# Two mixers of a float32 transformer: the input's projections as plain float32 matmuls instead of split ones

## The chip, the cores and the metric

The kernel runs on one core of one Trainium2 chip. The metric is the device time of one execution in microseconds (us). A core has five engines with a queue each: TensorE (PE in the rows; PEld is its weight load), VectorE (DVE), ScalarE (ACT), GpSimd (POOL) and SyncE (SP), whose queue issues nearly all DMAs here. Matmul results land in PSUM, in eight banks of 128x512 float32; everything else lies in SBUF.

## The reference, cut to what matters

A batch of one, 256 tokens of width 1024, float32 throughout. Two layers of a first block are followed by a second block that the change does not touch. Each layer of the first block is

```
mix = hybrid_mixer(x, w_in[l], ...)
x = layer_norm(ALPHA * x + mix)
ff = swiglu(x) if l == 0 else moe_swiglu(x)
x = layer_norm(ALPHA * x + ff)
```

and the mixer begins with one projection of its input, `proj = einsum('btd,de->bte', x, w_in)`, whose 3218 columns are cut into the queries, keys, values, decay, beta and gate of a gated delta rule (chunks of 64 tokens, 6 heads of 64), the two halves of a gated linear unit before a depthwise convolution over 31 tokens, and the queries, keys, values and forget gates of a causal attention. The three results are joined and multiplied by an output matrix.

## The kernel before

**Stages.** `build` runs mixer 0, a dense feed-forward, mixer 1 (both by `mixer1`), a mixture of experts, and the second block. Weights are packed on the host so that 1 MB (128 partitions x 2048 floats) is one DMA. `load` (L162) takes one of four `raw` slots in turn and issues that DMA on SP's queue, for all stages.

**The split.** TensorE has a one-pass form for operands rounded to float32r. To keep float32 accuracy, every operand is written as high + low part. `part` (L169) makes, from one half of a raw block, `wh` on ScalarE (L172, a copy that rounds) and `wl` on VectorE (L174, raw minus `wh`); three buffers of each. `mm3` (L181) then multiplies by three matmuls, high x high (L183), high x low (L184) and low x high (L185). The input is transposed by TensorE in `split_t` (L255) and split in the same way: `xTh` by ScalarE (L271), `xTl` by VectorE (L272).

**The projections in a mixer.** `proj_a` (L212) gives channels on partitions: per block two tiles of 128 channels, each eight groups of `mm3` over the 1024 inputs, with the weights stationary and 256 tokens moving. `proj_b` (L224) gives tokens on partitions: the input stationary, 256 weight columns moving. `proj_s` (L241) does as `proj_a` for the 18 small columns. A mixer has 19 channel tiles (`TILES_A`: k, q, v, the attention's f and g, and b and a of the gated linear unit), three blocks by `proj_b` (attention values, gates) and one by `proj_s`. All results go through two PSUM banks with the tag "a".

**Order of the work.** The source traces `proj_s`, three `pair_in` (k and q), `decays`, `pair_front`, `spare(3)` and `spare(4)` (values and one attention tile), then `inverse`, `scan`, `fox`, `conv` and `gates`. The framework's scheduler turns the trace into one order per engine: an instruction that is ready goes, and among ready ones the earlier in the source. So the projections in `fox`, `conv` and `gates` fill TensorE while the inverse waits for VectorE (`invert16`, L509 and L510: 15 dependent steps). Each engine then runs its list strictly in order.

**Near the change.** `conv` already multiplies plain float32 on TensorE: some of its 31 taps are diagonal 128x128 matrices against 256 tokens (`mm` at L362, tile `a_conv`); the other taps are VectorE's (L764). At the end of a mixer `split_t` makes the two parts `mT` of the joined result, which take the same buffers as `xTh` and `xTl`, and `proj_b` multiplies them by the output matrix, as before the change and after it.

Of the kernel before, what the change touches and what calls it, by code (L numbers as in the profile page):

```python
# [9 lines left out]
F32 = mybir.dt.float32  # L10
# [10 lines left out]
P = 128  # L21
D = 1024
KC = D // P
T = 256
# [79 lines left out]
class Net:  # L104
# [107 lines left out]
    def proj_a(self, src, xT, tiles=2, parts=None):  # L212
# [8 lines left out]
                self.mm3(ps[:, t, :], wh[:, k, :], wl[:, k, :], xh[:, k, :], xl[:, k, :], k == 0, k == 7)  # L221
        return ps

    def proj_b(self, src, xT, cols=256, nk=8, parts=None):  # L224

        xh, xl = xT
        ps = self.ps("a", "pB").rearrange("p (t n) -> p t n", t=2)
        k0 = 0
        for wh, wl in parts or self.weights(src, nk * cols):
            wh = wh.rearrange("p (k c) -> p k c", c=cols)  # L230
            wl = wl.rearrange("p (k c) -> p k c", c=cols)
            n = wh.shape[1]
            for t in range(2):
                for k in range(n):
                    s = slice(t * P, t * P + P)
                    self.mm3(ps[:, t, :cols], xh[:, k0 + k, s], xl[:, k0 + k, s], wh[:, k, :], wl[:, k, :],
                             k0 + k == 0 and t == 0, k0 + k == nk - 1)
            k0 += n
        return ps

    def proj_s(self, tag, src, xT, cols, sb):  # L241

        xh, xl = xT
        (wh, wl), = self.weights(src, 8 * cols)
        wh, wl = (w.rearrange("p (k c) -> p k c", c=cols) for w in (wh, wl))
        ps = self.ps("a", "pS")
        for k in range(8):
            self.mm3(ps[:cols, :T], wh[:, k, :], wl[:, k, :], xh[:, k, :], xl[:, k, :], k == 0, k == 7)
        self.nc.scalar.activation(sb, ps[:cols, :T], AF.Copy)
        ps = self.ps(tag, "pSt").rearrange("p (t n) -> p t n", t=2)  # L250
        for t in range(2):
            self.nc.tensor.transpose(ps[:, t, :cols], sb[:, t * P:t * P + P], self.ident[:cols, :cols])
        return ps[:, :, :cols]

    def split_t(self, tag, x, hl, kcs, gains=None, src0=0):  # L255

        nc = self.nc
        hi, lo = hl
        kcs = list(kcs)
        step = 2  # L260
        for b in range(0, len(kcs), step):
            sub = kcs[b:b + step]
            ps = self.ps(tag, "tr").rearrange("p (k t n) -> p k t n", k=2, t=2)
            for i, kc in enumerate(sub):
                for t in range(2):
                    o = (src0 + kc - kcs[0]) * P
                    nc.tensor.transpose(ps[:, i, t, :], x[:, t, o:o + P], self.ident)
            if gains is None:
# [85 lines left out]
    def mixer1(self, l, x, xT):  # L354
        nc, A, ident = self.nc, self.A, self.ident
        V, S, PE = nc.vector, nc.scalar, nc.tensor
        wA, wB, wS = A["w_in_a"], A["w_in_b"], A["w_in_s"]
# [12 lines left out]
        ps = self.proj_s("g", wS[l], xT, 18, mp.tile([18, T], F32, name="projs", tag="rowf"))  # L370
# [20 lines left out]
        ps = self.ps("g", "cum").rearrange("p (t n) -> p t n", t=2)  # L391
# [11 lines left out]
        rows = mp.tile([18, 2, T], F32R, name="rowsT")  # L403
        ps = self.ps("g", "rows")
# [24 lines left out]

        def pair_in(p):  # L430

            psj = self.proj_a(wA[l, p], xT)
            kq = kqs[p] = mp.tile([P, 2, T], F32, name=f"kq{p}")
            for i in range(2):
                conv4(kq[:, i, :], psj[:, i, :], 3 * i + p)
            sg = mp.tile([P, 2, T], F32, name="sg", bufs=3)
            self.sigmoid(sg, kq)
            V.tensor_tensor(kq, kq, sg, op=ALU.mult)
# [173 lines left out]
        def spare(c):  # L612

            names = TILES_A[2 * c:2 * c + 2]
            ps = self.proj_a(wA[l, c][:, :1024 * len(names)], xT, tiles=len(names))
            for i, n in enumerate(names):
                if n[0] == "v":
                    value(ps[:, i, :], int(n[1]))
                else:
                    S.activation({"b": glu[:, 0:2], "a": glu[:, 2:4], "f": foxqk[:, 0:3], "g": foxqk[:, 3:6]}[n[0]][:, int(n[1]), :],  # L620
                                 ps[:, i, :], AF.Copy)
# [12 lines left out]
        def fox():  # L634

            for c in FOXC:
                spare(c)
                yield
            ps = self.proj_b(wB[l, 0], xT)
            S.activation(fv[:, :, 0:256], ps, AF.Copy)  # L640
            yield
            ps = self.proj_b(wB[l, 1], xT)
            S.activation(fv[:, :, 256:384], ps[:, :, 0:128], AF.Copy)
            S.activation(gate[:, :, 0:128], ps[:, :, 128:256], AF.Copy)
            yield
            for t in range(2):
                n = P * (t + 1)
# [138 lines left out]

        def gates():
            gsg = late[3]
            ps = self.proj_b(wB[l, 2], xT)
            S.activation(gate[:, :, 128:384], ps, AF.Copy)  # L790
            self.sigmoid(gsg, gate)
            V.tensor_tensor(gate, gate, gsg, op=ALU.mult)
            yield
# [6 lines left out]
        for c in range(2):  # L800
            g = msc[:, 3 + c:4 + c]
# [37 lines left out]
        self.normed = self.rsqrt(rs, mv[:, :, 1], 1.0, 1e-5)  # L839
        return mv, rs  # L840

    def layer_norm_T(self, tag, r, st, rows, n=4):

        V = self.nc.vector
        mv, rs = self.moments(r, st, n)
        xT = self.new_xT()
        for h in range(2):
            s = slice(h * 512, h * 512 + 512)
            for t in range(2):
                V.scalar_tensor_tensor(r[:, t, s], r[:, t, s], mv[:, t, 0:1], rows[:, 0, s], op0=ALU.subtract, op1=ALU.mult)  # L850
                V.scalar_tensor_tensor(r[:, t, s], r[:, t, s], rs[:, t:t + 1], rows[:, 1, s], op0=ALU.mult, op1=ALU.add)
            self.split_t(tag, r, xT, range(4 * h, 4 * h + 4), src0=4 * h)
        return xT

    def layer_norm_T_first(self, tp, tag, r, st, rows, name, n=4):

# [35 lines left out]
        return r  # L892

    def to_T(self, tag, x):
        xT = self.new_xT()
        self.split_t(tag, x, xT, range(8))
        return xT

    def residual_ffn1(self, fp, l, x, xT, spare):
        A, nc = self.A, self.nc  # L900
# [951 lines left out]
def build(tc, A, out):  # L1852
    with ExitStack() as ctx:
# [13 lines left out]
            r, st = net.residual_ffn1(fp, 0, r, xT, net.prepare2(fp))  # L1867
        with net.banks(a=2, g=4, f=2), pool("mix1") as net.mp:
            rows = net.load_rows(net.mp.tile([P, 2, D], F32, name="rows", tag="lb"), "ln_ffn", 0, 2)
            xT = net.layer_norm_T("g", r, st, rows, 2)  # L1870
            r, st = net.mixer1(1, r, xT)
        with net.banks(a=4, y=2, t=2), pool("moe") as fp:
            rows = net.load_rows(fp.tile([P, 2, D], F32, name="rows"), "ln_mix", 2, 2)
# [34 lines left out]
```

## Time and profile before

| | us |
|---|---|
| median of 3 runs (2184.49 to 2192.83) | 2185.77 |
| the profiled execution, its own time | 2192.82 |
| its span, first to last instruction | 2191.0 |
| TensorE matmul busy in the span | 2060.1 |
| VectorE busy | 1294.7 |
| ScalarE busy | 1024.0 |
| mean granted TensorE clock, share of full | 0.968 |

The profile is one execution, recorded by the hardware. A row of a window gives, for each engine, the busy time and the count of its instructions; PEclk is the granted clock of TensorE as a share of 2.4 GHz. Matmuls overlap, so their durations add up to more than the time that they take; the distance between two starts tells what one costs. A row of the waits names the engine, line and tile that waited, and what released it.

### The profile page before, as it was taken

The numbers are of one execution on the slowest core, as the hardware profiler recorded it, in microseconds if no ns is written. First come the engines' busy times: TensorE is split into PE (matmuls) and PEld (weight loads), VectorE is DVE, ScalarE is ACT, GpSimd is POOL, SyncE is SP. The second block draws the span as 40 slices with busy tenths as digits, with TensorE's granted clock in tenths as the row PEclk, the third lists the DMA queues.
The fourth block names the chain that finished last, engine by engine and source line by source line (L and its number), as shares of the span: only waits on it lengthen the run. The fifth ranks groups of instructions, "written<-read, shape, count | busy, mean of one in ns | idle before, by whom it ended". The sixth has DMA issues, their size and how long they took to land. (4 is left out here: it accounts for less than half of the span.)

```text
span 2191.0 us, 31905 instructions
## 1 busy us (share of the span) xinstructions
PE 2060.1 (94%) x12770; PEld 1610.7 (74%) x12770; DVE 1294.7 (59%) x1903; ACT 1024.0 (47%) x1448; POOL 13.0 (1%) x27
## 2 busy tenths in 40 slices
PE   8998999899979999998899999987799999999998
PEld 7877999788768888432377785322699988878997
DVE  6768954666668998300288985000555568665554
ACT  6445444464547777200177774000544444554443
POOL 0000000000000000000000000000000000000000
PEclk9979999998989999999999999999899999999999
DMA  6313675322459999899999999999455553444552
GB/s 234 106 40 117 216 259 175 135 87 98 167 188 338 359 340 352 321 425 425 426 426 417 348 347 364 425 426 424 182 183 191 180 196 126 135 163 154 179 187 97
DMA packets 78988, 545.36 MB, mean 249 GB/s; under 512 B 8961, under 2 KB 11273, under 8 KB 13937
## 3 DMA queue, kind: packets, MB, share of 16 engines
q1 hardware_dynamic: 76112, 527.40, 64.2%
q0 software_dynamic: 2720, 15.84, 1.9%
q8 instruction: 103, 1.69, 0.3%
q14 instruction: 53, 0.43, 0.1%
HBM read 536.72 MB, written 6.49 MB: 248 GB/s over the span
## 5 line engine op out<-in xcount | busy, mean ns | idle before, releaser
L174 DVE TENSOR_TENSOR wl<-raw,wh 128x1024 fp32r<-128x1024 f32 (+1 forms) x662 | 799.2, 1218 | 378.5 <-ACT wh L172 375.0
L172 ACT ACTIVATE wh<-raw 128x1024 fp32r<-128x1024 f32 (+1 forms) x662 | 694.2, 1055 | 602.8 <-PE a_pA L184 272.8
L183 PE MATMUL a_pA<-xTh,wh 128*128 128x256 f32 x1456 | 420.7, 290 | 6.2 <-ACT foxqk L620 3.5
L185 PE MATMUL a_pA<-xTh,wl 128*128 128x256 f32 x1456 | 416.7, 287 | 0.7 <-DVE wl L174 0.7
L184 PE MATMUL a_pA<-xTl,wh 128*128 128x256 f32 x1456 | 417.1, 287 | 0.2 <-DVE xTl L875 0.2
L183 PEld LDWEIGHTS a_pA<-xTh,wh 128*128 128x128 f32 x1456 | 282.4, 194 | 14.8 <-ACT foxqk L620 5.6
L184 PEld LDWEIGHTS a_pA<-xTl,wh 128*128 128x128 f32 x1456 | 282.6, 194 | 4.9 <-issue 3.2
L185 PEld LDWEIGHTS a_pA<-xTh,wl 128*128 128x128 f32 x1456 | 282.4, 194 | 3.6 <-issue 2.4
L1032 PE MATMUL a_up<-raw,xef 128*64 128x512 f32 x896 | 218.8, 597 | 26.3 <-DMA raw<-in_moe_w_dram 26.2
L1037 DVE TENSOR_TENSOR mos<-mos,a_up 128x512 f32<-128x512 f32 x42 | 28.7, 683 | 267.6 <-PE a_up L1032 258.7
L1032 PEld LDWEIGHTS a_up<-raw,xef 128*64 128x64 f32 x896 | 68.5, 136 | 154.9 <-issue 105.4
L184 PE MATMUL a_up<-wl,xeh 128*128 128x512 f32 x448 | 180.3, 403 | 1.9 <-DVE wl L174 1.8
L185 PE MATMUL a_up<-wh,xel 128*128 128x512 f32 x448 | 178.0, 397 | 0.0
L183 PE MATMUL a_up<-wh,xeh 128*128 128x512 f32 x448 | 175.8, 399 | 0.0
L183 PE MATMUL a_pB<-wh,xTh 128*128 128x256 f32 x480 | 140.9, 295 | 5.6 <-ACT glu L620 3.2
L184 PE MATMUL a_pB<-wl,xTh 128*128 128x256 f32 x480 | 139.0, 290 | 0.0
L1065 PE MATMUL y_y<-raw,mof 128*64 128x512 f32 x448 | 131.8, 600 | 7.5 <-DMA raw<-in_moe_w_dram 7.4
L185 PE MATMUL a_pB<-wh,xTl 128*128 128x256 f32 x480 | 137.7, 289 | 1.1 <-DVE xTl L278 0.9
L184 PEld LDWEIGHTS a_up<-wl,xeh 128*128 128x128 f32 x448 | 84.7, 189 | 28.3 <-DVE wl L174 6.8
L1036 ACT ACTIVATE mos<-a_up 128x512 f32<-128x512 f32 x42 | 24.7, 587 | 171.0 <-PE a_up L1032 168.7
L185 PE MATMUL acc_acc<-wh,ffl 128*128 128x512 f32 x264 | 102.0, 392 | 0.0
L184 PE MATMUL acc_acc<-wl,ffh 128*128 128x512 f32 x264 | 102.0, 392 | 0.0
(559 smaller groups left out, 2774.0 us busy)
## 6 DMA issues: line engine op xcount, KB each, us to landing
raw<-in_moe_w_dram SPq DMA_DIRECT2D x336, 1024.0 KB, 10.8
raw<-in_ffn_in_dram SPq DMA_DIRECT2D x44, 1024.0 KB, 4.9
raw<-in_ffn_w_dram SPq DMA_DIRECT2D x33, 1024.0 KB, 4.9
raw<-in_w_in_a_dram SPq DMA_DIRECT2D x24, 1024.0 KB, 4.9
raw<-in_ffn_out_dram SPq DMA_DIRECT2D x22, 1024.0 KB, 4.9
raw<-in_w_out_dram SPq DMA_DIRECT2D x12, 1024.0 KB, 4.9
raw<-in_w_in_g_dram SPq DMA_DIRECT2D x12, 1024.0 KB, 5.0
raw<-in_w_in_b_dram SPq DMA_DIRECT2D x6, 1024.0 KB, 4.9
```

Of the source, the lines that this page charges most:

```text
L172: nc.scalar.activation(wh[:, :m], raw[:, o:o + m], AF.Copy)
L174: nc.vector.tensor_tensor(wl[:, :m], raw[:, o:o + m], wh[:, :m].bitcast(F32), op=ALU.subtract)
L183: mm(out, lh, rh, start=start, stop=False, skip_group_check=True)
L184: mm(out, lh, rl, start=False, stop=False, skip_group_check=True)
L185: mm(out, ll, rh, start=False, stop=stop, skip_group_check=True)
L1032: PE.matmul(ps[r], xe[0][:, k0, r], w[:, k * 512:k * 512 + 512], start=k0 == 0, stop=k0 == 7, skip_group_check=True)
L1036: self.last = S.activation(s, pp[0], AF.Silu)
L1037: V.tensor_tensor(s, s, pp[1], op=ALU.mult)
L1065: PE.matmul(py[h][r], hf[:, k, r], w[:, j * 1024 + h * 512:j * 1024 + h * 512 + 512], start=b == 0 and k == 0, stop=b == 6 and k == 3, ski ...
```

## The change

In both mixers every projection of the input takes the raw weight block and an unsplit transposed input, as plain float32 operands: one matmul in place of three, and no `part`. `plain_a`, `plain_b` and a second branch in `proj_s` do this; `to_T` and `layer_norm_T(..., flat=True)` make the one transposed input `xTf`, in the buffer of `xTl`, with its copies alternately on VectorE and ScalarE. The output projection of the mixers, the feed-forward, the experts and the second block keep the split form.

```diff
+    def plain_a(self, src, xf, tiles=2):
+
+        raw = self.load(src, 1024 * tiles).rearrange("p (t k c) -> p t k c", t=2, k=8)
+        ps = self.ps("a", "pA").rearrange("p (t n) -> p t n", t=2)
+        for t in range(tiles):
+            for k in range(8):
+                self.nc.tensor.matmul(ps[:, t, :], raw[:, t, k, :], xf[:, k, :], start=k == 0, stop=k == 7, skip_group_check=True)
+        return ps
+
+    def plain_b(self, src, xf):
+
+        raw = self.load(src).rearrange("p (k c) -> p k c", k=8)
+        ps = self.ps("a", "pB").rearrange("p (t n) -> p t n", t=2)
+        for t in range(2):
+            for k in range(8):
+                self.nc.tensor.matmul(ps[:, t, :], xf[:, k, t * P:t * P + P], raw[:, k, :], start=k + t == 0, stop=k == 7, skip_group_check=True)
+        return ps
...
+            w = self.load(src, 8 * cols)[:, :8 * cols].rearrange("p (k c) -> p k c", c=cols)
+            for k in range(8):
+                self.nc.tensor.matmul(ps[:cols, :T], w[:, k, :], xT[:, k, :], start=k == 0, stop=k == 7, skip_group_check=True)
...
+            if lo is None:
+                (nc.scalar.copy if b % 4 else nc.vector.tensor_copy)(hi[:, sub[0]:sub[0] + len(sub), :], ps[:, :len(sub)].rearrange("p k t n -> p k (t n)"))
...
-            psj = self.proj_a(wA[l, p], xT)
+            psj = self.plain_a(wA[l, p], xT)
...
-            ps = self.proj_a(wA[l, c][:, :1024 * len(names)], xT, tiles=len(names))
+            ps = self.plain_a(wA[l, c][:, :1024 * len(names)], xT, len(names))
...
-            ps = self.proj_b(wB[l, 0], xT)
+            ps = self.plain_b(wB[l, 0], xT)
...
-            ps = self.proj_b(wB[l, 1], xT)
+            ps = self.plain_b(wB[l, 1], xT)
...
-            ps = self.proj_b(wB[l, 2], xT)
+            ps = self.plain_b(wB[l, 2], xT)
...
-        xT = self.new_xT()
-        self.split_t(tag, x, xT, range(8))
+        xT = self.flat_xT()
+        self.split_t(tag, x, (xT, None), range(8))
         return xT
+
+    def flat_xT(self):
+        return self.ap.tile([P, 8, T], F32, name="xTf", tag="xTl")
...
-            xT = net.layer_norm_T("g", r, st, rows, 2)
+            xT = net.layer_norm_T("g", r, st, rows, 2, flat=True)
```

## Rows read from the trace of the kernel before

**Rows 1.** Windows of both mixers: length; busy PE, PEld, DVE, ACT, POOL; clock, DMA, GB/s.

```profile
9.80:176.50 166.70, 157.70 (x1445) 133.13 (x1443) 118.76 (x286) 89.71 (x197) 0.86 (x2) 0.91 0.30 107
415.70:584.10 168.40, 161.30 (x1453) 136.31 (x1451) 113.61 (x268) 88.88 (x195) 0.53 (x1) 0.89 0.26 89
```

**Rows 2.** Windows of 10 us, columns as above.

```profile
60.00:70.00 10.00, 8.42 (x67) 7.44 (x60) 9.97 (x28) 1.60 (x3) 0.00 (x0) 0.83 0.31 107
80.00:90.00 10.00, 8.42 (x70) 8.22 (x70) 8.73 (x28) 6.29 (x14) 0.00 (x0) 1.00 0.31 107
120.00:130.00 10.00, 10.00 (x71) 6.44 (x71) 4.88 (x14) 2.78 (x10) 0.00 (x0) 0.55 0.01 2
130.00:140.00 10.00, 10.00 (x86) 7.07 (x82) 5.23 (x17) 3.94 (x15) 0.00 (x0) 0.50 0.00 1
140.00:150.00 10.00, 10.00 (x87) 7.78 (x88) 5.07 (x16) 3.96 (x13) 0.00 (x0) 0.59 0.01 2
...
540.00:550.00 10.00, 10.00 (x70) 6.77 (x64) 4.03 (x12) 4.21 (x15) 0.00 (x0) 0.50 0.01 2
```

**Rows 3.** Waits of TensorE in mixer 1: total us, times, longest.

```profile
PE a_pA L183 <- ACT foxqk L620: 1.8, 2, 1.6
PE a_pB L183 <- ACT glu L620: 1.6, 1, 1.6
PE f_cvar L362 <- ACT glu L772: 1.2, 1, 1.2
PE a_pA L183 <- ACT wh L172: 1.2, 1, 1.2
PE g_tr L267 <- DVE mixed L816: 0.9, 2, 0.6
```

**Rows 4.** Line 183 in mixer 1: ns min/median/max, first and last start.

```profile
L183 PE MATMUL a_pA<-xTh,wh x152: 275/283/682, 416.1 to 524.8; 128*128 128x256 f32 x152
...
L183 PE MATMUL a_pB<-wh,xTh x49: 278/283/563, 495.8 to 584.1; 128*128 128x256 f32 x49
...
L183 PE MATMUL a_pS<-xTh,wh x8: 276/282/562, 415.7 to 420.4; 128*18 128x256 f32 x8
```

**Rows 5.** Timeline of TensorE in mixer 0, ends of a run: start, us.

```profile
21.18 0.28 PE L183 MATMUL a_pA<-xTh,wh 128*128 128x256 f32 x1
...
25.38 0.28 PE L185 MATMUL a_pA<-xTh,wl 128*128 128x256 f32 x1
```

**Rows 6.** The same timeline around one tap of the convolution.

```profile
160.37 0.28 PE L185 MATMUL a_pB<-wh,xTl 128*128 128x256 f32 x1
160.49 0.59 PE L362 MATMUL a_conv<-cup,dgt 128*128 128x256 f32 x2
160.74 0.47 PE L183 MATMUL a_pB<-wh,xTh 128*128 128x256 f32 x1
161.04 0.28 PE L184 MATMUL a_pB<-wl,xTh 128*128 128x256 f32 x1
```

**Rows 7.** Windows of lines 174 (VectorE), 172 (ScalarE) alone, mixer 1.

```profile
415.70:584.10 168.40, 31.77 (x26) 0.89 0.26 89
...
415.70:584.10 168.40, 27.49 (x26) 0.89 0.26 89
```

**Rows 8.** VectorE's groups in mixer 0: count, busy us, mean ns.

```profile
L272 DVE TENSOR_TENSOR xTl<-g_tr,xTh 128x512 fp32r<-128x512 f32 x4 | 2.8, 690 | 1.3 <-ACT xTh L271 1.3
```

**Rows 9.** DMA issues: count, size, median us from issue to landing.

```profile
raw<-in_w_in_a_dram SPq DMA_DIRECT2D x24, 1024.0 KB, 4.9
```

**Rows 10.** Windows of the inverse's steps: line 174 alone, then all engines.

```profile
80.50:105.90 25.40, 7.33 (x6) 1.00 0.42 131
...
80.50:105.90 25.40, 23.82 (x189) 22.54 (x189) 21.60 (x61) 12.17 (x25) 0.00 (x0) 1.00 0.42 131
```

**Rows 11.** Weight loads: line 183 in mixer 1, line 362 in both.

```profile
L183 PEld LDWEIGHTS a_pA<-xTh,wh x152: 186/192/338, 415.9 to 524.7; 128*128 128x128 f32 x152
...
L362 PEld LDWEIGHTS a_conv<-cup,dgt x56: 186/192/337, 122.4 to 574.7; 128*128 128x128 f32 x56
```

More of the change, by code (lines that the diff above doesn't have):

```diff
@@ L241, in proj_s @@
     def proj_s(self, tag, src, xT, cols, sb):
-        xh, xl = xT
-        (wh, wl), = self.weights(src, 8 * cols)
-        wh, wl = (w.rearrange("p (k c) -> p k c", c=cols) for w in (wh, wl))
         ps = self.ps("a", "pS")
-        for k in range(8):
-            self.mm3(ps[:cols, :T], wh[:, k, :], wl[:, k, :], xh[:, k, :], xl[:, k, :], k == 0, k == 7)
+        if isinstance(xT, tuple):
+            xh, xl = xT
+            (wh, wl), = self.weights(src, 8 * cols)
+            wh, wl = (w.rearrange("p (k c) -> p k c", c=cols) for w in (wh, wl))
+            for k in range(8):
+                self.mm3(ps[:cols, :T], wh[:, k, :], wl[:, k, :], xh[:, k, :], xl[:, k, :], k == 0, k == 7)
+        else:
+            w = self.load(src, 8 * cols)[:, :8 * cols].rearrange("p (k c) -> p k c", c=cols)
+            for k in range(8):
+                self.nc.tensor.matmul(ps[:cols, :T], w[:, k, :], xT[:, k, :], start=k == 0, stop=k == 7, skip_group_check=True)
         self.nc.scalar.activation(sb, ps[:cols, :T], AF.Copy)
@@ L267, in split_t @@
                     nc.tensor.transpose(ps[:, i, t, :], x[:, t, o:o + P], self.ident)
-            if gains is None:
+            if lo is None:
+                (nc.scalar.copy if b % 4 else nc.vector.tensor_copy)(hi[:, sub[0]:sub[0] + len(sub), :], ps[:, :len(sub)].rearrange("p k t n -> p k (t n)"))
+            elif gains is None:
                 k0, n = sub[0], len(sub)
@@ L840, in moments, with layer_norm_T @@
         return mv, rs
-    def layer_norm_T(self, tag, r, st, rows, n=4):
+    def layer_norm_T(self, tag, r, st, rows, n=4, flat=False):
         V = self.nc.vector
         mv, rs = self.moments(r, st, n)
-        xT = self.new_xT()
+        xT = (self.flat_xT(), None) if flat else self.new_xT()
         for h in range(2):
@@ L852, in layer_norm_T @@
             self.split_t(tag, r, xT, range(4 * h, 4 * h + 4), src0=4 * h)
-        return xT
+        return xT[0] if flat else xT
     def layer_norm_T_first(self, tp, tag, r, st, rows, name, n=4):
@@ L894, in to_T @@
     def to_T(self, tag, x):
-        xT = self.new_xT()
-        self.split_t(tag, x, xT, range(8))
-        return xT
+        xT = self.flat_xT()
+        self.split_t(tag, x, (xT, None), range(8))
+        return xT
+    def flat_xT(self):
+        return self.ap.tile([P, 8, T], F32, name="xTf", tag="xTl")
     def residual_ffn1(self, fp, l, x, xT, spare):
```

## The prediction

> **What bounds the kernel now.** I began with the windows over the two mixers, since the change touches nothing else. The first runs from its first projection to the first output projection, 166.7 us, the second likewise, 168.4 us [rows 1]. TensorE is busy for 157.7 and 161.3 us of them, VectorE for 118.8 and 113.6, ScalarE for 89.7 and 88.9. So TensorE has about 9.0 and 7.1 us without work, and the reader should see that it is the full resource. The last columns say that it did not run at full speed all the time: the granted clock averages 0.91 and 0.89. As it takes only two levels, 2.4 and 1.2 GHz, the loss against full clock is at most 0.09 x 166.7 + 0.11 x 168.4 = 15.0 + 18.5 = 33.5 us.
>
> The windows of 10 us show where [rows 2]. In the front TensorE has few gaps (8.4 of 10 us busy from 60 to 70 and from 80 to 90, with VectorE at 10.0 and 8.7). From 120 to 150 it is busy all the time at a clock of 0.55, 0.50 and 0.59, and 540 to 550 in the second mixer looks the same. VectorE and ScalarE are half idle there, so TensorE sets the pace at half clock, with small matmuls of the chunk inverse, the forgetting attention and the depthwise convolution.
>
> Then the waits of TensorE in the second mixer [rows 3]: 1.8 + 1.6 us for ScalarE to empty a projection's PSUM bank, 1.2 us for a split weight. The first mixer has the same three rows with the same numbers: 9.2 us in both.
>
> **The change, part by part.**
>
> *Matmuls.* A group of three matmuls (one 128x256 weight block against all 256 tokens) becomes one in plain float32. The second mixer has 152 + 48 + 8 = 208 groups [rows 4] (the 49th pB record is the output projection's first), the first as many by the code. In a full run of projections the starts go from 21.18 to 25.38 us over 36 records [rows 5]: 4.20 / 35 = 0.120 us each, 0.360 us a group. Plain float32 of exactly this shape stands in the kernel already, in the convolution's taps. Between the single-pass matmuls that start at 160.37 and 161.04 lie one tap (two records) and one single-pass matmul [rows 6]: 0.67 = 0.120 + tap + 0.120, so 0.43 us for a tap. So TensorE gets 0.43 - 0.36 = 0.07 us more per group; with the tap at 0.434 from the same rows and 0.120 not rounded further, 0.074 x 416 = **+30.8 us** in both mixers. Where the clock is halved the addition doubles.
>
> The Trainium skill, "FP8 and Floating Point Precision" (TensorE Precision Notes), counts true float32 as four passes through the array, where the trace shows the split form to take three; by 4/3 a group would be an estimated 0.48 us, and the sum +50 instead of +31. The tap rows contradict it by a tenth, so the sum goes by them.
>
> *Splits.* In the second mixer 26 weight halves of 128x1024 no longer pass ScalarE (27.5 us) and VectorE (31.8 us) [rows 7]; the first has 26 of its 28 splits in the projections. Neither engine is the full one, so this is worth only the waits that end on them: the 9.2 us above at most, nothing at least, since a PSUM bank can still be late. With a third of its work gone ScalarE will mostly be in time: **-8 us**. At the mixers' ends TensorE waits for VectorE's and ScalarE's normalisations (1.2 us for glu, 0.9 us for mixed in the second [rows 3]); VectorE reaches them with less in its queue: **-2 us** over both, between 0 and -4.
>
> *Clock.* The rows of before cannot show the mixture of after. Neither a gain nor a loss is excluded: projections now stay longer on TensorE and can stand among the small matmuls, as between 80 and 90, where the clock is 1.00, or they can be used up before and leave the same stretch. The stretches at half clock of 120 to 150 and 530 to 560 hold most of the 33.5 us; between 0 and -33.5 I take **-13**, two fifths, a little nearer to nothing: the window with projections throughout, 80 to 90, is at 1.00, but the single taps among the small matmuls did not lift 0.50 [rows 2].
>
> *Input transposed once.* Four batches of 128x512 are now copied once, on VectorE and ScalarE in turn, in place of a copy and a subtraction (0.69 us [rows 8]). I cost this at nothing: the first projections run while the last transposes are still going. Without that cover one subtraction per mixer, 1.4 us in all, would be gained.
>
> *Loads.* No load is added. A raw slot is now freed by the last matmul of its block, not by the two splits, so on SP's queue the next load is issued later, and all loads of later stages stand behind it. With four slots, three blocks of 16 x 0.434 = 6.9 us lie between, 20.8 us, against 4.9 us to landing [rows 9]. Nothing on the path; if only one slot were ahead it would still be covered. ScalarE's DMA and POOL's queue are not touched. The new transposed tile sits in the buffer that the output projection's second operand takes later; it frees after the last gate projection, as before.
>
> *Sum.* +30.8 - 8 - 2 - 13 = +7.8 us. The profiled execution took 2192.82 us (span 2191.0, 1.8 around it), 0.3% over the median of the runs, 2185.77. The durations are its own; the difference goes on either: 2200.6 against the profiled execution, **2194 us** against the median. No measurement of this kernel tells less than about 0.5% (11 us) from no change.
>
> **Rivals.**
>
> *A, slower: the clock stays low and the projections slide into it.* Place: 120 to 150 and 530 to 560. For it: taps of the same plain form stand there and the clock was 0.50 all the same; in-order TensorE cannot skip them. It decides once the gates' and gated-linear projections are ready before the inverse's small matmuls and are issued ahead of them or are used up early. The clock gives back nothing and half of the waits stay: 30.8 - 4 = +27, 2213 us. Against it: VectorE's lighter load brings the small matmuls earlier, among the projections.
>
> *B, faster: the inverse's chain sets the end, not TensorE's sum.* Between 80.5 and 105.9 us VectorE works through 15 dependent steps of the inverse; six splits of 1.22 us stand among them, 7.3 us, and as many in the second mixer [rows 10]. If everything behind hangs on this chain, both mixers end 14.7 us sooner, and the extra 30.8 us of TensorE find room in its gaps (9.0 + 7.1) and in the clock's loss (33.5): 2171 us. For it: VectorE is busy 21.6 of these 25.4 us. Against it: TensorE is busy 23.8 of them.
>
> *C, faster: weight loads set TensorE's pace.* A weight load takes 0.192 us, in the split form and for the taps alike [rows 11]; three per group become two. If loads were the pace at 0.120 us each, a group would fall to 0.24 and 416 groups would give -50, with the waits 2127 us. The tap rows speak against it: two loads, but 0.43 us between starts. In the Trainium skill, "Perfetto Trace Analysis" (Identifying the Most-Contended Engine) has TensorE judged by the busy share of its weight loads and not by that of its matmuls; by that rule this change would relieve the engine. The trace does not agree, because the starts of the taps lie further apart than their loads last.
>
> **How the numbers follow.** The forecast, part of the clock given back, has 0.47; its own range is 2184 to 2202, from two thirds of the clock's loss given back to one seventh. A has 0.27, B 0.23, C 0.03. Of the forecast 0.36 lies within 0.5%, 0.11 above. A gives 0.22 slower and 0.05 the same, B 0.21 faster and 0.02 the same, C 0.03 faster. Together: faster 0.24, same 0.43, slower 0.33. For eight in ten the range goes to the centres of A and B and a little beyond, 2167 to 2216; the outer halves of A and B are left out for the most part, and C.
>
> **What would show it.** Right: starts of the plain projections two records and 0.43 us apart; splits in the mixers gone, so VectorE about 64 and ScalarE 55 us less busy in all; no wait of TensorE for wh; both mixers 166.7 and 168.4 us long give or take 10, with the clock above 0.91 and 0.89. The forecast is wrong if the projections stand closer than 0.40 us apart (C), if the mixers are over 12 us longer each at an unchanged clock (A), or if the inverse's steps take some 18 us instead of 25.4 and the mixers end sooner by as much (B).

## The result, and the profile after

The changed kernel takes 2202.94 us (median of 4 runs, 2200.24 to 2205.40) beside 2186.75 us for the kernel before in the same comparison: a ratio of 1.0066, interval 1.0042 to 1.0089, slower by 0.7%. The forecast was 2194 us, with no difference that can be told as the likeliest case. The profiled execution took 2205.40 us, 12.6 us more than that of before, and its span is 2203.4 us. Executions of one kernel differ, and their time goes with the clock: 77 others of the kernel before, run beside the experiments, took from 2177 us at a mean granted clock of 0.976 to 2195 us at 0.966, so its profiled one (2192.82 us at 0.968) is among the long ones.

The page's first part and four of its groups (line, engine, operation, tiles, count; busy us, mean ns; idle time before and its releaser), after:

```profile
PE 2077.0 (94%) x12354; PEld 1602.0 (73%) x12354; DVE 1238.0 (56%) x1847; ACT 973.6 (44%) x1392; POOL 12.8 (1%) x27
...
L174 DVE TENSOR_TENSOR wl<-raw,wh 128x1024 fp32r<-128x1024 f32 x610 | 737.4, 1220 | 350.8 <-ACT wh L172 347.7
L172 ACT ACTIVATE wh<-raw 128x1024 fp32r<-128x1024 f32 x610 | 640.7, 1057 | 535.1 <-PE a_pA L184 229.0
...
L230 PE MATMUL a_pA<-xTf,raw 128*128 128x256 f32 x608 | 145.8, 394 | 0.0
...
L183 PE MATMUL a_pB<-wh,xTh 128*128 128x256 f32 x384 | 112.5, 294 | 12.1 <-ACT xTh L827 11.6
```

VectorE is 1294.7 - 1238.0 = 56.7 us and ScalarE 1024.0 - 973.6 = 50.4 us less busy, so the splits are gone. The last row holds what is new: the output projections' first kind of matmul has 12.1 us of idle time before it, and 11.6 us of that ends with ScalarE's line 827. That line writes the convolution's part of the joined result (two of its eight blocks of 128 channels) into the output projection's operand.

The windows tell where it counts. After, mixer and output projection of either block in turn (length; busy PE, PEld, DVE, ACT, POOL; granted clock, DMA, GB/s), with the feed-forward stage between:

```profile
10.20:180.90 170.70, 166.25 (x1225) 129.19 (x1225) 89.03 (x253) 64.20 (x166) 0.54 (x1) 0.93 0.30 105
180.90:214.90 34.00, 27.46 (x203) 26.74 (x202) 21.17 (x40) 15.34 (x24) 1.64 (x3) 0.88 0.43 149
214.90:425.90 211.00, 198.55 (x1377) 184.94 (x1375) 143.26 (x250) 93.11 (x117) 3.38 (x6) 0.97 0.55 189
425.90:590.60 164.70, 163.08 (x1234) 126.30 (x1233) 85.99 (x240) 63.93 (x166) 0.52 (x1) 0.97 0.29 102
590.60:623.30 32.70, 27.50 (x201) 27.04 (x202) 16.02 (x29) 11.79 (x19) 0.01 (x1) 0.90 0.69 263
```

The kernel before, the stages that [rows 1] leave out, output projection, feed-forward stage, output projection:

```profile
176.50:202.60 26.10, 25.99 (x192) 25.51 (x192) 19.11 (x35) 13.32 (x20) 1.48 (x3) 0.89 0.57 204
202.60:415.70 213.10, 198.18 (x1376) 184.46 (x1375) 145.75 (x253) 96.24 (x122) 3.38 (x6) 0.97 0.57 197
...
584.10:610.50 26.40, 24.14 (x192) 23.32 (x192) 14.57 (x26) 9.46 (x14) 0.00 (x0) 1.00 0.85 323
```

Against [rows 1] the mixers, up to their first output projection, are 4.0 us longer and 3.7 us shorter: +0.3 us together. The output projections went from 26.1 and 26.4 to 34.0 and 32.7 us, +14.2, and the stage between gave 2.1 back. So in these two executions the whole loss stands behind the point at which the prediction let the mixers end. Of the 14.2 us, 9.4 are time in which TensorE stands idle (6.5 and 5.2 after, 0.1 and 2.3 before); the other 4.8 are longer busy time, from matmuls of the norm and transposes that now stand in this stretch and from the clock (0.88 and 0.90 after 0.89 and 1.00). TensorE's waits there, first block and then second, after:

```profile
PE a_pB L183 <- ACT xTh L827: 6.4, 1, 6.4
```

```profile
PE a_pB L183 <- ACT xTh L827: 5.2, 1, 5.2
```

The longest there before, first block and then second:

```profile
PE a_pB L183 <- ACT xTh L277: 0.7, 1, 0.7
```

```profile
PE a_pB L183 <- ACT xTh L802: 1.4, 1, 1.4
```

L802 before is the same line as L827 after. The timelines follow the convolution back. Its product (gated-linear projections times their gate) in the first and the second mixer, before and then after:

```profile
118.58 0.68 DVE L748 TENSOR_TENSOR cup<-glu 128x512 f32<-128x512 f32 x1
...
527.46 0.69 DVE L748 TENSOR_TENSOR cup<-glu 128x512 f32<-128x512 f32 x1
```

```profile
141.79 0.69 DVE L773 TENSOR_TENSOR cup<-glu 128x512 f32<-128x512 f32 x1
...
178.66 0.69 DVE L790 TENSOR_TENSOR ccv<-ccv,a_conv 128x512 f32<-128x512 f32 x1
...
554.72 0.68 DVE L773 TENSOR_TENSOR cup<-glu 128x512 f32<-128x512 f32 x1
```

The product comes 23 and 27 us later (17 us in the second mixer, whose start moved by 10). VectorE adds up its taps until the last sum, which starts at 178.66 us. Then TensorE, first block:

```profile
179.40 2.07 PE L387 MATMUL f_cmean<-ccv,ones 128*128 128x256 f32 x4
180.91 0.78 PE L183 MATMUL a_pB<-wh,xTh 128*128 128x256 f32 x1
...
183.97 1.02 PE L387 MATMUL f_cvar<-glu,ones 128*128 128x256 f32 x4
184.83 1.17 PE L290 MATMUL f_tr<-call,mixed 128*128 128x128 f32 x6
192.41 0.58 PE L183 MATMUL a_pB<-wh,xTh 128*128 128x256 f32 x1 [6.41 <-ACT xTh L827]
```

The convolution's norm starts at 179.4 us, the output projection begins at 180.9 with the rows of the joined result that it has, runs out of them, and stands for 6.4 us until the norm's chain has gone through VectorE and ScalarE (13 us from its first matmul to 192.4).

### The profile page after: what moved, and what is told of

Read it like the earlier page. It is cut to its first block, busy times and chain, and to the rows that moved or that the text cites. A ratio compares the mean times of both kernels' runs of the same rounds, so it can differ in the third digit from the quotient of the medians.

```text
span 2203.4 us, 30896 instructions
## 1 busy us (share of the span) xinstructions
PE 2077.0 (94%) x12354; PEld 1602.0 (73%) x12354; DVE 1238.0 (56%) x1847; ACT 973.6 (44%) x1392; POOL 12.8 (1%) x27
## 5 line engine op out<-in xcount | busy, mean ns | idle before, releaser
L174 DVE TENSOR_TENSOR wl<-raw,wh 128x1024 fp32r<-128x1024 f32 x610 | 737.4, 1220 | 350.8 <-ACT wh L172 347.7
L172 ACT ACTIVATE wh<-raw 128x1024 fp32r<-128x1024 f32 x610 | 640.7, 1057 | 535.1 <-PE a_pA L184 229.0
L183 PE MATMUL a_pA<-xTh,wh 128*128 128x256 f32 x1152 | 326.8, 285 | 0.7 <-DVE xTl L303 0.5
L185 PE MATMUL a_pA<-xTh,wl 128*128 128x256 f32 x1152 | 326.4, 284 | 0.5 <-DVE wl L174 0.5
L184 PE MATMUL a_pA<-xTl,wh 128*128 128x256 f32 x1152 | 326.7, 284 | 0.0
L183 PEld LDWEIGHTS a_pA<-xTh,wh 128*128 128x128 f32 x1152 | 221.3, 193 | 3.0 <-DVE xTl L303 0.7
L184 PEld LDWEIGHTS a_pA<-xTl,wh 128*128 128x128 f32 x1152 | 221.3, 192 | 2.5 <-issue 1.2
L185 PEld LDWEIGHTS a_pA<-xTh,wl 128*128 128x128 f32 x1152 | 221.2, 192 | 1.7 <-issue 0.9
L230 PE MATMUL a_pA<-xTf,raw 128*128 128x256 f32 x608 | 145.8, 394 | 0.0
L230 PEld LDWEIGHTS a_pA<-xTf,raw 128*128 128x128 f32 x608 | 117.4, 197 | 23.7 <-issue 8.4
L183 PE MATMUL a_pB<-wh,xTh 128*128 128x256 f32 x384 | 112.5, 294 | 12.1 <-ACT xTh L827 11.6
## 6 DMA issues: line engine op xcount, KB each, us to landing
raw<-in_moe_w_dram SPq DMA_DIRECT2D x336, 1024.0 KB, 10.6
raw<-in_ffn_in_dram SPq DMA_DIRECT2D x44, 1024.0 KB, 4.8
raw<-in_ffn_w_dram SPq DMA_DIRECT2D x33, 1024.0 KB, 4.9
raw<-in_w_in_a_dram SPq DMA_DIRECT2D x24, 1024.0 KB, 4.9
raw<-in_ffn_out_dram SPq DMA_DIRECT2D x22, 1024.0 KB, 4.8
raw<-in_w_out_dram SPq DMA_DIRECT2D x12, 1024.0 KB, 4.8
raw<-in_w_in_g_dram SPq DMA_DIRECT2D x12, 1024.0 KB, 4.9
raw<-in_w_in_b_dram SPq DMA_DIRECT2D x6, 1024.0 KB, 4.8
```

The lines of the kernel that those rows point to most:

```text
L172: nc.scalar.activation(wh[:, :m], raw[:, o:o + m], AF.Copy)
L174: nc.vector.tensor_tensor(wl[:, :m], raw[:, o:o + m], wh[:, :m].bitcast(F32), op=ALU.subtract)
L183: mm(out, lh, rh, start=start, stop=False, skip_group_check=True)
L184: mm(out, lh, rl, start=False, stop=False, skip_group_check=True)
L185: mm(out, ll, rh, start=False, stop=stop, skip_group_check=True)
L230: self.nc.tensor.matmul(ps[:, t, :], raw[:, t, k, :], xf[:, k, :], start=k == 0, stop=k == 7, skip_group_check=True)
```

## Experiments

Three readings were open: that the loss is the convolution's late part (theory 1), that the sum of TensorE's work sets the time and the wait is only where it shows (theory 2), and that the relief of VectorE and ScalarE is worth much or little (theory 3). Each comparison has its own runs of the kernel before, whose median moved between 2181 and 2187 us, so ratios are compared where a per cent matters.

**The product ahead of the attention.** The gated-linear projections and their product are written behind the delta rule's scan instead of behind the attention.

```diff
-FOXC, GLUC = (5, 6, 7), (8, 9)
+FOXC, GLUC = (5, 6), (7, 8, 9)
...
-        self.emit(inverse(), scan(), fox(), conv(), gates())
+        cg = conv()
+        self.emit(inverse(), scan())
+        next(cg)
+        self.emit(fox(), cg, gates())
```

> The changed kernel with the gated-linear tiles, and the product of their halves, traced before the attention instead of behind it; the same work. Theory 1 (the end is late because these projections were used as late filler, so that the convolution's taps on VectorE end last): the product comes before 125 us in mixer 0 instead of 141.8, TensorE waits under 2 us for the convolution's half of the output projection instead of 6.4 and 5.2, and the time falls by 8 to 14 us, to 2189 to 2195. Theory 2 (the added TensorE time alone sets the end, in any order): within 4 us of the changed kernel, 2199 to 2207.

Measured: 2193.54 us, ratio 1.0024 (0.9999 to 1.0049). The product came at 90.1 us, the wait for the convolution went (the longest wait left in the first output projection is 0.4 us), and 9 us of the 16 came back.

```profile
90.06 0.69 DVE L773 TENSOR_TENSOR cup<-glu 128x512 f32<-128x512 f32 x1 [0.20 <-ACT glu L645]
```

The work now stands among the inverse's steps, whose last one moved from 99.7 to 116.5 us, and the first mixer is 175.4 us long. Theory 1 holds so far, but the edit moves another chain too.

**The same order on the kernel before.**

> The kernel before with the same tiles traced earlier: the control for the order alone. Theory 1: there the product came at 118.6 us and the convolution was not the last by much, so within 5 us of the kernel before, 2182 to 2192. Theory 2 says the same. If it gains as much as the changed kernel does, the order is a gain of its own and tells nothing of the change.

Measured: 2209.09 us, ratio 1.0106 (1.0082 to 1.0130), against the expectation. Its mixers, same columns:

```profile
9.70:189.70 180.00, 165.86 (x1444) 141.53 (x1442) 119.25 (x291) 91.45 (x202) 0.56 (x2) 0.84 0.28 99
427.80:600.00 172.20, 158.69 (x1453) 135.76 (x1451) 114.86 (x276) 90.96 (x201) 0.53 (x1) 0.91 0.25 87
```

They are 13.3 and 3.8 us longer than in [rows 1]; the clock fell to 0.84 in the first. In the split form the inverse, on a fuller VectorE, ends at 128.0 us instead of 105.3 when the product's work stands among its steps. The same order thus has opposite worth in the two kernels.

**The splits put back, their results unused.** The projections stay plain; the 50 halves that the plain projections load are split all the same, and nothing reads the result (the small projections' halves are not put back).

```diff
-        raw = self.load(src).rearrange("p (k c) -> p k c", k=8)
+        raw = self.load(src)
+        for o in (0, 1024):
+            self.part(raw, o)
+        raw = raw.rearrange("p (k c) -> p k c", k=8)
```

(and likewise in the other plain projection)

> The changed kernel with ScalarE and VectorE splitting every projection weight again (the wide blocks, 50 halves; the 18 small columns are left out), into buffers that nobody reads; TensorE's work is that of the changed kernel. This undoes the relief and keeps the price. Theory 1 and 2 both hold the relief for secondary: 0 to 8 us slower than the changed kernel, 2203 to 2211. A rival theory 3, that the relief of 32 us of VectorE per mixer paid for most of the added 31 us: 15 us slower or more, over 2218.

Measured: 2230.79 us, ratio 1.0208 (1.0188 to 1.0229), 28 us over the changed kernel; 0 to 8 had been expected. Its mixers:

```profile
10.00:189.90 179.90, 168.71 (x1235) 129.86 (x1234) 117.94 (x281) 88.01 (x196) 0.69 (x2) 0.94 0.28 98
433.20:616.10 182.90, 172.51 (x1242) 132.32 (x1241) 107.76 (x260) 82.12 (x187) 0.54 (x1) 0.93 0.29 102
```

They are 9.2 and 18.2 us longer than in the changed kernel, and TensorE stands idle for 11.2 and 10.4 us instead of 4.4 and 1.6. So taking the splits away is worth some 28 us, and the plain matmuls without it cost 45. The prediction had kept this relief to the waits that end on a split or a bank; most of it does not appear there. Part of it is seen in the chains: with the splits back the inverse's last step starts at 111.34 us instead of 99.68, and TensorE's wait for the layer norm before the second mixer is 12.8 us instead of 7.6 (9.7 in the kernel before). In the second mixer the clock is 0.93 instead of 0.97. How much each of these makes up was not separated.

**The convolution's rows in a second pass of the output projection.** A block first multiplies its six other rows in both weight halves, then the convolution's two (`proj_late`, not shown here, is `proj_b` in this order).

```diff
-            ps = self.proj_b(A["w_out"][l, c], mT)
+            ps = self.proj_late(A["w_out"][l, c], mT, (0, 1, 2, 5, 6, 7, 3, 4))
```

> The changed kernel with the output projection summing over the convolution's rows (3 and 4 of 8) last, in a first pass of six and a second of two per block; the same matmuls. Theory 1: two blocks' first passes, 72 matmuls at 0.12 us, 8.6 us, now cover the wait for the convolution where 18 did, so the waits of 6.4 and 5.2 us mostly go: 6 to 11 us faster than the changed kernel, 2192 to 2197. Theory 2: no change beyond 3 us.

Measured: 2212.44 us, ratio 1.0108 (1.0077 to 1.0139), no faster where 6 to 11 us less was expected. The wait for the convolution shrank to 1.2 us, but waits for split weights took its place, in the first output projection:

```profile
PE a_pB L184 <- DVE wl L174: 3.4, 3, 1.5
PE a_pB L183 <- ACT wh L172: 1.4, 2, 0.8
PE a_pB L183 <- ACT xTh L841: 1.2, 1, 1.2
```

A second pass holds both halves of a block until its end, and there are only three buffers for halves; that this is why the weights came late is read from the code and was not tried by itself.

**The product right behind the attention's last values**, between the place that it has and that of the first experiment. (The expectation calls the place the forget gate's projection; the block there, the second by `plain_b`, holds the attention's last values and the delta rule's first output gates. The forget gates are among the 18 small columns.)

```diff
+            next(cg)
+            yield
...
-        self.emit(inverse(), scan(), fox(), conv(), gates())
+        cg = conv()
+        self.emit(inverse(), scan(), fox(cg), cg, gates())
```

> The changed kernel, with the gated-linear tiles and their product asked for right behind the attention's forget gate's last projection, ahead of the attention's softmax: between the changed kernel (product at 141.8 us) and the first experiment (product at 90.1 us, which put the inverse's last step back from 99.7 to 116.5 us). Theory 1 (the convolution's late half is what costs, 6.4 and 5.2 us of waits at the output projections): the product comes between 95 and 125 us in the first mixer, both waits fall below 1.5 us, the inverse ends before 110 us, and the time is 2185 to 2195 us. Theory 2 (the sum of TensorE's work sets the time wherever the product stands): 2199 to 2206 us, with the waits gone but as much idle time elsewhere in the mixers.

Measured: 2204.08 us, ratio 1.0081 (1.0057 to 1.0104). The product came at 124.8 us, the inverse's last step stayed at 99.9, and yet nothing was gained where 2185 to 2195 us had been expected. The product and the sums of the taps, on VectorE:

```profile
124.83 0.69 DVE L775 TENSOR_TENSOR cup<-glu 128x512 f32<-128x512 f32 x1
...
164.05 0.69 DVE L792 TENSOR_TENSOR ccv<-ccv,a_conv 128x512 f32<-128x512 f32 x1 [0.20 <-PE a_conv L387]
```

and TensorE in the same execution:

```profile
175.87 2.36 PE L387 MATMUL f_fo<-fv,fpT 128*128 128x64 f32 x18
178.06 1.08 PE L387 MATMUL f_cmean<-ccv,ones 128*128 128x256 f32 x4
...
189.57 0.58 PE L183 MATMUL a_pB<-wh,xTh 128*128 128x256 f32 x1 [6.42 <-ACT xTh L830]
```

The sums were there at 164.7 us, but the norm's first matmul starts at 178.06, directly behind the attention's last output matmuls, and the wait is 6.4 us as before. The tiles' names tell why that could be: both begin with f_, so both take their PSUM banks from the same family of two, in the order in which they are written down, and the attention stands first.

**The convolution's rows last in the packed weights.** The rows of w_out are permuted where they are packed, so that these two are the last of the second half, and no weight is held longer (the mixer's writes into `mT` and their gains follow the same order, not shown).

```diff
-    out["w_out"] = pack_b(I["w_out"])
+    wo = I["w_out"]
+    out["w_out"] = pack_b(np.concatenate([wo[:, 0:384], wo[:, 640:1024], wo[:, 384:640]], 1))
```

> The changed kernel, with the rows of the output projection's weights put in another order when they are packed, so that the convolution's two rows of the joined result are the last ones that each block multiplies, in the second weight half, with the weights held no longer than before. Nothing of the mixer's own order is touched. Theory 1: the first block can multiply its six other rows (some 18 matmuls of 0.12 us and their first weights) before the convolution's half is wanted, so the waits of 6.4 and 5.2 us shrink by 2 to 6 us each, and the time is 2191 to 2199 us. Theory 2: the waits are only renamed (the block's weights, or its sums' buffers, come to be waited for as in the run that multiplied these rows in a second pass), and the time is 2200 to 2210 us.

Measured: 2207.30 us, ratio 1.0091 (1.0059 to 1.0123). The waits fell to 2.5 us each, as theory 1 wanted, and the time lies where theory 2 put it. From the mixer's start to the last output matmul the first block took 200.0 us (204.7 in the changed kernel), the second 201.2 (197.4), its mixer at a clock of 0.94 instead of 0.97. Together that is 0.9 us less than in the changed kernel. That this span is 6.2 us longer all the same comes from behind the second output projection, from work that the edit does not touch (some 1586 us instead of 1580). Inconclusive by itself.

**Both of these edits**, the product behind the attention's last values and the rows last in the packed weights.

> Both of the two edits above together. Theory 1: the convolution's half is in time once the product is earlier, so the rows' order adds under 3 us to what the product's place gives: 2183 to 2194 us, at or a little under the kernel before. Theory 2: 2199 to 2210 us. If the two edits sum (each worth 6 us or more beyond the other), the waits were two separate ones and theory 1 in its present form is too simple.

Measured: 2192.38 us, ratio 1.0027 (1.0007 to 1.0047). Each alone gave nothing, together they gave 10 us, although by theory 1 the rows' order should have added under 3 us to the other edit. The waits for the convolution are 2.5 us each, and the norm still starts directly behind the attention's last output matmuls (178.39 us). Two things could keep the convolution's part late, one behind the other: the product's place and then the bank. The next run takes the bank away.

**The norm out of the attention's banks**, with the product behind the attention's last values:

```diff
-            ps = self.ps("f", "cmean")
+            ps = self.ps("g", "cmean")
...
-            ps = self.ps("f", "cvar")
+            ps = self.ps("g", "cvar")
```

> The kernel of the run that asked for the product right behind the forget gate's projection, with one thing more: the sums of the convolution's norm are placed in the accumulator banks of the delta rule's family (four banks) and no longer in the attention's family (two banks). In that run the convolution's sums were complete at 164.1 us in the first mixer, but the first matmul of its norm started at 178.1 us, 0.1 us behind the attention's last output matmul (177.9 us); in the second mixer 586.6 us behind 586.5 us. Theory 1b (the convolution's half has two things to wait for, its late product and then the attention's banks, and each alone is enough to keep it late): the norm starts within 5 us of the sums' end, the waits of 6.4 and 5.2 us at the output projections fall below 1.5 us, and the time is 2188 to 2197 us. Rival (the order in which the work is queued keeps the norm late, and the banks have nothing to do with it): the norm still starts behind the attention's last matmul, the waits stay, and the time is 2200 to 2207 us.

Measured: 2186.99 us, ratio 1.0024 (1.0007 to 1.0042), 17 us less by the medians (0.6% by the ratios) than without the two letters, and 1 us under the expected range. The sums and then TensorE, first mixer:

```profile
160.03 0.68 DVE L792 TENSOR_TENSOR ccv<-ccv,a_conv 128x512 f32<-128x512 f32 x1
```

```profile
161.19 1.13 PE L387 MATMUL g_cmean<-ccv,ones 128*128 128x256 f32 x4
...
172.30 1.00 PE L387 MATMUL f_fo<-fv,fpT 128*128 128x64 f32 x8
```

The norm now starts 0.5 us behind the end of the sums (160.71 us) and 11 us ahead of the attention's last matmuls. Mixer and output projection of either block:

```profile
9.90:171.50 161.60, 160.64 (x1221) 125.25 (x1221) 90.53 (x258) 64.27 (x169) 0.54 (x1) 0.98 0.32 112
171.50:196.40 24.90, 24.83 (x208) 24.57 (x207) 19.14 (x35) 14.05 (x23) 1.54 (x3) 1.00 0.57 199
407.20:570.40 163.20, 162.99 (x1243) 127.36 (x1242) 85.53 (x239) 65.21 (x168) 0.54 (x1) 0.98 0.27 92
570.40:600.30 29.90, 26.22 (x195) 25.28 (x192) 15.89 (x30) 10.66 (x17) 0.00 (x0) 0.89 0.88 352
```

The wait of 6.4 us is gone, 2.0 of the 5.2 are left (under 1.5 had been expected), and TensorE is busy for all but 1.0 and 0.2 us of the mixers. This is theory 1 with its second step: the late product, and then the shared bank. The expectation's rival, that the order and not the bank keeps the norm late, falls. Not all of the gain is the wait: the mean clock of the runs is 0.977 (median of ten) where it was 0.973 without the two letters.

**The same with the convolution's rows last.**

> The same two letters (the convolution's norm in the delta rule's banks) on the kernel with both the earlier product and the convolution's rows last in the output projection, which measured 2192.4 us and still had waits of 2.5 us at both output projections and its norm behind the attention's last matmul. Theory 1b: the 2.5 us waits go in both mixers, and the time is 2184 to 2191 us, no more than 5 to 8 us under that kernel. Rival: the norm stays where it is, 2190 to 2196 us.

Measured: 2189.45 us, ratio 1.0026 (1.0007 to 1.0045): in the expected range, and nothing beyond the run above. The waits of 2.5 us are gone, but once the norm is early the rows' order has nothing more to hide.

**The two letters alone.**

> The changed kernel with the two letters alone, its order otherwise untouched. There the convolution's sums end at 178.7 us, 10 us behind the attention's last output matmul (168.9 us), so the bank is free long before it is wanted. Theory 1b: no difference, the norm starts at 179 to 180 us, waits of 5 to 7 us at the output projections stay, 2199 to 2206 us. If it is 2195 us or less, the bank was a cost in the changed kernel itself, and the product's late place was not the first cause.

Measured: 2208.04 us, ratio 1.0111 (1.0073 to 1.0149), 2 us over the expected range. No gain, as theory 1 said, since the bank is not what the norm waits for while the sums end at 181 us. It moved the wait: TensorE now reaches the norm before the sums are there, and 2.5 us of the old wait stay. In the first block:

```profile
PE g_cmean L387 <- DVE ccv L790: 5.9, 1, 5.9
PE a_pB L183 <- ACT xTh L827: 2.5, 1, 2.5
```

**Both edits on the kernel before.**

> The kernel before, split projections and all, with the two edits that brought the changed kernel from 2203 to 2187 us (the product right behind the forget gate's projection, the convolution's norm in the delta rule's banks). Theory 1b: the two edits mend a lateness that the plain projections made; before them the convolution's half was 3.9 and 4.9 us behind the first output projection, and nothing waited for it, so there is nothing to mend. An earlier product takes filler from the inverse's end, as the run that moved it ahead of the inverse showed (2209 us), but less of it: 2183 to 2200 us, no faster than the kernel before by more than 0.3%. Rival (the edits are a gain of their own, whatever the projections are): 2165 to 2177 us, and then the change itself costs 10 us or more even where its order suits it.

Measured: 2177.54 us, ratio 0.9956 (0.9936 to 0.9975). The kernel before gains too, 0.4%, which theory 1 had not expected; the expectation's rival, a gain of the edits whatever the projections are, is missed by half a us. It has hardly such a wait to lose (0.7 and 1.4 us); its mixers show what it gained:

```profile
9.90:167.60 157.70, 151.62 (x1445) 130.90 (x1443) 116.74 (x283) 88.86 (x194) 0.53 (x1) 0.95 0.32 113
410.30:568.80 158.50, 153.28 (x1453) 131.71 (x1451) 113.30 (x268) 87.98 (x195) 0.53 (x1) 0.94 0.24 82
```

The granted clock rose from 0.91 and 0.89 [rows 1] to 0.95 and 0.94. By the prediction's reckoning the loss to the clock fell from 33.5 to 0.05 x 157.7 + 0.06 x 158.5 = 17.4 us, so of the 18.9 us by which the mixers are shorter at most 16 are clock. TensorE's busy time there, with as many matmuls, fell by 14.1 us.

**The first edit alone on the kernel before.**

> The kernel before with the first of the two edits alone (the product right behind the forget gate's projection), the convolution's norm left in the attention's banks. With both edits it measured 2177.5 us, and its trace showed 17 us of half clock in each mixer where the kernel before had 32 and 36 us. If the gain on the split kernel is the product's place, by the clock (the convolution's taps on TensorE and VectorE stand in a stretch that was left thin), this run gives 2174 to 2181 us, with 25 us or less of half clock in each mixer. If it takes both, as on the changed kernel (2204 us with the first edit alone), the norm starts right behind the attention's last output matmul, and the time is 2182 to 2190 us.

Measured: 2175.97 us, ratio 0.9963 (0.9944 to 0.9982), the same as with both. The norm does start right behind the attention's last matmul there, and 5.2 us of wait appear at the first output projection, but the mixers more than make up for it:

```profile
9.90:166.80 156.90, 150.20 (x1435) 129.54 (x1433) 116.00 (x280) 87.26 (x191) 0.53 (x1) 0.95 0.32 113
411.60:566.40 154.80, 148.21 (x1453) 127.61 (x1451) 112.00 (x266) 87.50 (x194) 0.53 (x1) 0.98 0.27 89
```

These are single executions; over all runs the mean granted clock is 0.9775 here (median of ten) and 0.972 in the kernel before beside it (thirteen), which on 2180 us is some 12 us, and the medians are 9.8 us apart. So on the split kernel it is the product's place that pays, through the clock; on the plain one it takes both edits, through the wait and in part the clock.

None of these versions with plain projections is faster than the kernel before; the best are at 1.0024. The kernel before with the product moved is at 0.9963.

## Why the prediction was right or wrong

The measured 2202.94 us lies inside the stated 2167 to 2216, 9 us over the forecast and 1 us beyond the forecast's own range of 2184 to 2202. The terms show how much of that is luck.

**The matmuls' price: right.** A full run of plain projections after:

```profile
38.32 4.91 PE L230 MATMUL a_pA<-xTf,raw 128*128 128x256 f32 x22
```

With 0.39 us for the last one, (4.91 - 0.39) / 21 = 0.215 us lie between two records, and as a matmul leaves two of them, 0.43 us between matmuls, as the taps had said. A longer run, 44 records from 21.76 us on that take 9.76 us, gives 0.218, so 0.43 to 0.44: some +30 us over 416 groups. Rival C falls with it: a group loads two weights now instead of three, and TensorE's time rose. The Trainium skill's four passes ("FP8 and Floating Point Precision", TensorE Precision Notes) would have been 0.48 us by the prediction's estimate; the trace shows 0.43 us, so the measurement decides for the taps' row.

**The splits' waits: right as far as they went.** The waits on foxqk, glu and wh [rows 3] are gone from both mixers, -9.2 us where -8 was taken. VectorE and ScalarE gave back 56.7 and 50.4 us for 64 and 55. But the splits put back cost 28 us, so what their absence is worth is three times the waits that end on them, in this order of the work. Without that the change would have been slower by about 2%.

**The clock: right in the profiles, in part by luck.** 0.93 and 0.97 leave 0.07 x 170.7 + 0.03 x 164.7 = 16.9 us of the 33.5, a gain of 16.6 where 13 was taken. But the profiled execution of the kernel before has a mean clock of 0.968 over its span, where the 77 others have 0.972 in the median; the changed kernel's four have 0.974. From 0.968 to 0.974 is some 13 us of the span, from 0.972 some 4. So by the medians the clock gives back less than the term says, and rival A, which had it give back nothing, falls in the profiles but is not excluded over all runs. Where in the span the other executions lose or gain their clock is not on record.

**The sum up to the first output projection: near.** +30 - 9.2 - 16.6 = +4 us, measured +0.3. The clock is read to two decimals, which leaves some 0.8 us open in each of its four products; what makes up the rest was not separated.

**The step that failed: "At the mixers' ends TensorE waits for VectorE's and ScalarE's normalisations ... with less in its queue: -2 us over both, between 0 and -4."** The waits that it names came to about nothing: the one for mixed went from 2.3 to 4.3 us in the first mixer and from 0.9 to 0.3 in the second, and the 1.2 us for glu no longer appear. What came is a wait that it does not name, 6.4 and 5.2 us for the convolution's rows, and output projections that are 14.2 us longer. The step looked at what VectorE has in its queue and not at what starts the convolution: the product of the gated-linear projections, which the order uses as late filler. It slid back by 17 to 23 us, and the convolution, some 37 us of taps and 13 us of norm, has no cover behind it. The prediction ended each mixer at its first output projection, though only part of the joined result has to be there by then, and named nothing that would be late next. With +14.2 for -2 the sum would have been +24 on the terms as taken and +18 on the terms as measured. The profiles differ by 12.6 us, since the mixers came out 4 us under their terms and the stage between gave 2.1 back: TensorE's wait for the layer norm before the second mixer fell from 9.7 to 7.6 us, relief that the prediction did not count. The medians differ by 16.2. So it is partly luck that the time lies as near as it does: an omission of 16 us met smaller errors of the other sign. Why the written order and the scheduler put the product that much later was not tried; that it is the product's place and then the bank is shown by the runs with one edit, the other, and both.

**Rival B's sign appeared, and B did not.** The inverse's steps on VectorE, first and behind the last, after:

```profile
85.78 0.17 DVE L534 TENSOR_TENSOR w<-lb,x 128x24 f32<-128x24 f32 x1
...
99.68 0.49 DVE L536 TENSOR_TENSOR u<-x,call 128x384 f32<-128x384 f32 x1
```

They took 13.9 us, less than the 18 that B asked for, and their last one came 5.6 us earlier (105.3 us before); the first mixer was still 4 us longer. The chain was relieved and did not set the end.

**What the change is worth where its order suits it.** Both kernels gain about 0.4% from the two edits, for different reasons: 1.0066 to 1.0024 (the two intervals touch at 1.0042), and 1.0000 to 0.9956. With the edits in both, the plain form is slower by 1.0024 / 0.9956 = 1.0068, about as much as without; the medians, from two comparisons, lie 9 us apart and the ratios 15, as the medians of the kernel before in the two are 2181.07 and 2185.12 us. So the late convolution says where the time went in this kernel, but the price does not vanish when it is mended, and there theory 2, the added work of TensorE, stands: the split kernel has a reserve of its own, its low clock, that the same edits reach. In the profiles, mixers up to the first output projection, the price is 324.8 - 316.2 = 8.6 us. The terms give +30 for the matmuls, -9.2 for the waits, and for the clock 6.5 - 17.4 = -10.9, +9.9 in all, which goes with the medians; the 5 us that the ratios hold beyond that are within the intervals.

## What to carry to other kernels

Where a change relieves one engine and lengthens work that serves as filler, follow each branch that joins behind the stage back to what starts it, and name which would be late next; the end of a stage is where the last branch joins, not where its first consumer starts. If an earlier start of a branch gains nothing, look at whose buffers its next step shares and in which order they are handed out. Before a wait found in the changed kernel is called the change's cost, make the same mending edit on the kernel before: it may gain as much.

## What was not expected of the hardware

In this kernel TensorE's clock follows the order of the work as much as the form of the matmuls. Over whole runs the split kernel's mean granted clock is 0.972 as written (median of thirteen), 0.9775 with one product moved (ten) and 0.9605 with it moved further, ahead of the attention (four), with the same matmuls and loads; the change to plain projections made it 0.974 (four). In the profiles' mixers that is 0.91 and 0.89, then 0.95 and 0.98, then 0.84 and 0.91. The stretch at half clock of the kernel before (0.55, 0.50 and 0.59 from 120 to 150 us [rows 2]), taken by the prediction as something that plain projections might or might not mend, grew short without them. The same three windows of the split kernel with the product moved:

```profile
120.00:130.00 10.00, 10.00 (x147) 8.75 (x148) 9.54 (x28) 6.91 (x26) 0.00 (x0) 1.00 0.01 3
130.00:140.00 10.00, 10.00 (x135) 8.10 (x134) 9.76 (x25) 4.29 (x15) 0.00 (x0) 0.93 0.31 107
140.00:150.00 10.00, 10.00 (x45) 7.08 (x46) 4.56 (x12) 4.19 (x10) 0.00 (x0) 0.73 0.00 1
```

TensorE is busy throughout in both, before and here.
